# Taking the sorted experts of a mixture in the order narrow, wide, wide, narrow, wide, wide, narrow

## The chip, the cores and the metric

The kernel runs on one core of one Trainium2 chip. The metric is the device time of one execution in microseconds (us). Three runs of the kernel before gave 1553.4, 1556.64 and 1560.38 us; the median is 1556.64 us. The profiled execution took 1559.97 us, of which 1558.3 us lie between its first and its last instruction (the span).

## The reference

The program is a decoder trunk of two layers on 256 tokens of 1024 features, all in 32-bit floats. Each layer mixes the tokens (a gated convolution, a state-space model, two kinds of attention) and then mixes channels. The channel mixer of layer 0 is dense; the one of layer 1 sends each token to two of eight experts. Only that last part bears on the change:

```python
logits = (h @ router_w).astype(jnp.float32)
top_val, top_idx = lax.top_k(logits, 2)
top_w = jax.nn.softmax(top_val, axis=-1)
gate = jnp.sum(jax.nn.one_hot(top_idx, 8) * top_w[..., None], axis=-2)
for e in range(8):
    out = out + gate[..., e:e + 1] * swiglu(h, w_gate[e], w_up[e], w_down[e])
# swiglu(h, g, u, d) = (silu(h @ g) * (h @ u)) @ d, with 1024 -> 3584 -> 1024
```

The weights of one expert are 3 x 1024 x 3584 numbers of 4 bytes, which is exactly 42 MiB (44.04 MB); all eight are 336 MiB. Every expert's weights are read once, whatever the number of its tokens.

## The kernel before, in words

Layer 0 and the token mixing of layer 1 fill the first 630 us or so of the span; the change does not touch them. The mixture of experts is `moe`, and its main loop runs over eight places `e` (L1405).

**Sorting and sizes.** Place 0 is always expert 0. The other seven experts are sorted on the chip by the number of their tokens, fullest first (`sort`, L1325); `order["ids"]`, `order["sl"]` and `order["ge"]` hold their numbers, the places of their tokens and their gates in that order. Expert 0 and the first four of the sorted ones (`WIDE`) have room for 96 tokens, the last three for 64. A place with 96 is called wide here, and one with 64 narrow. Tokens beyond the room would go to a part behind the loop (`beyond`), which runs only where there are any.

**Gather.** `gather` (L1185) collects the tokens of one or more experts: a matrix of zeros and ones `So` is built by VectorE, and 32 matmuls (L1204) multiply it with the tokens (in a high and a low part), so that X holds the tokens' columns side by side. Expert 0 is gathered ahead of the loop, with 96 columns. Three joint gathers serve the rest: behind the third unit of place 0 (for two experts), of place 2 (for two) and of place 4 (for three).

**Units.** An expert's 3584 hidden features are worked in four units `u`: three of 1024 features and one of 512. `hidden` (L1243) takes eight steps `k` over the 1024 input features. In each step one load of 1 MiB (half a load in the last unit) is multiplied with X; TensorE's columns are used in four strips of 32 tokens, so a step has 12 matmuls on strips for a wide place (`ROUNDS[3]`) and 8 for a narrow one (`ROUNDS[2]`). A 32-bit matmul is two instructions in the trace, so 24 and 16 records. `finish` (L1387) is the second half of a unit: `turn` transposes the hidden features (L1275, and L1282 for wide), `down` (L1286) multiplies them with 14 loads of 1 MiB for each expert (L1306 for wide, L1299 for narrow), and behind the last unit `gated` and `scatter` add the result to the output `y` (L1215 to L1226). `finish` is a generator, and `step(k)` takes one piece of it behind each step of a later `hidden` (two pieces behind the last two steps). A place's units have 43 pieces in all and its steps take 40, so the pieces run late, by three more at each place; what is left at the end is run behind the last `hidden`.

**Loads.** `load` (L261) issues each MiB on SyncE's queue, in the order of the program, into a ring of twelve places: nine tiles `raw` and the tiles `yA`, `sp` and `mix`. A load waits until the last matmul on the place's old contents is done. Twelve loads are 12/42 of an expert.

**Banks.** PSUM has two banks `ps` and six banks `acc`. A wide place takes two `acc` banks for its output and three for a unit of `hidden`; a narrow one takes one and two. The compiler's scheduler assigns them as they come free.

Of the kernel before, what the change touches and what calls it, by code (L numbers as in the profile page):

```python
# [10 lines left out]
F32R = mybir.dt.float32r  # L11
# [6 lines left out]
T, D, E = 256, 1024, 8  # L18
KD = D // 128
NT = T // 128  # L20
WIDE = 4
PI = math.pi
MAGIC = 12582912.0
C1 = 6.28125
# [141 lines left out]
def trunk(ctx: ExitStack, tc: tile.TileContext, I, out):  # L166
    nc = tc.nc
# [7 lines left out]
    def nm(n):  # L175
        cnt[0] += 1
        return f"{n}_{cnt[0]}"

    def st(shape, tag, bufs=1, dt=F32):
        return sb.tile(shape, dt, tag=tag, bufs=bufs, name=nm(tag))  # L180

    def s2(shape, dt=F32):
        return st(shape, "s2", NS2, dt)

    def bank(tag="acc"):
        return ps.tile([128, 512], F32, tag=tag, bufs=NPS[tag], name=nm(tag))

    def ts(o, a, s1, s2=None, op0=OP.mult, op1=None, eng=None):
        if s2 is None:
            (eng or V).tensor_scalar(o, a, s1, None, op0=op0)  # L190
        else:
            (eng or V).tensor_scalar(o, a, s1, s2, op0=op0, op1=op1)

    def tt(o, a, b, op=OP.mult):
        return V.tensor_tensor(o, a, b, op=op)  # L195

    def stt(o, a, s, b, op0=OP.mult, op1=OP.add):
        return V.scalar_tensor_tensor(o, a, s, b, op0=op0, op1=op1)  # L198

    def act(o, a, f, **k):  # L200
        S.activation(o, a, f, **k)  # L201
# [4 lines left out]
    x = st([128, KD, T], "x")  # L206
# [10 lines left out]
    def C(n):  # L217
        o, w = CS[n]
        return cst[:, o:o + w]
# [20 lines left out]
    hpi = st([128, 1], "hpi")  # L240
    V.memset(hpi, PI / 2)

# [56 lines left out]
    def run(*gens):  # L299
        for g in gens:  # L300
            for _ in g:
                pass
# [98 lines left out]
    def reduce2pi(r, a, n):  # L401
        ts(n, a, 1.0 / (2 * PI), MAGIC, OP.mult, OP.add)
        ts(n, n, MAGIC, None, OP.subtract)
        stt(r, n, -C1, a)
        stt(r, n, -C2, r)
        ts(r, r, PI, -PI, OP.min, OP.max)

# [89 lines left out]
    def rstd(src_ss, n, width, scale):  # L497
        ms = st([128, n], "ms", 2)
        pn = src_ss.shape[0]
        m = ms[:pn, :width]  # L500
        ts(m, src_ss, scale, 1e-6, OP.mult, OP.add)
        G.tensor_tensor(m, m, mhalf[:pn, :width], op=OP.pow)
        return ms
# [47 lines left out]
    def norm(l, which, shift, scale, old=None, lo=0, hi=KD):  # L551
        gs = gain(l, which, scale, lo, hi)
        rB, ah, al = old or (scales()[0], st([128, KD, T], "ah", 1, F32R), st([128, KD, T], "al", 1, F32R))
        u = gained(gs, lo, hi)
        for k2 in range(lo // 2, hi // 2):
            tt(u[k2], u[k2], rB[:, None, :].to_broadcast([128, 2, T]))
            for kk in range(2):
                k = 2 * k2 + kk
                act(ah[:, k], u[k2][:, kk], AF.Identity, bias=shift[:, k:k + 1])
                last = stt(al[:, k], u[k2][:, kk], shift[:, k:k + 1], ah[:, k].bitcast(F32), OP.add, OP.subtract)  # L560
        return rB, ah, al, last.ins

    def hop(n, l):
        for _ in range(1 + PAUSE.get((n, l), 0)):
            yield
# [6 lines left out]
    def mixer(l, ah, al, extra=(), second=None, ahead=None):  # L572
# [48 lines left out]
        def s5():  # L621
# [11 lines left out]
            yield  # L633
            W = [bank(), bank()]
            for ri in range(2):
                for i in range(8):
                    PE.matmul(W[ri][:, i * 64:(i + 1) * 64], BT[:, ri, i], U[:, i], start=True, stop=True)
            yield from hop("s51", l)
            W = [w.rearrange("p (i j) -> p i j", i=8) for w in W]
            a0, a1, a2, a3 = (s2([128, 8, 64]) for _ in range(4))  # L640
            tt(a0, W[0], cT)
            tt(a1, W[1], sT)
            tt(a2, W[1], cT)
            tt(a3, W[0], sT)
# [122 lines left out]
        def rope_norm(dst, src, tabs, g, tmp):  # L767
# [4 lines left out]
            act(m1[:pn], src, AF.Square)  # L772
            V.tensor_reduce(ss[:pn, :n], m1[:pn], axis=AX.X, op=OP.add)
            r = rstd(ss[:pn, :n], 8, n, 1.0 / 64)
# [91 lines left out]
        def sparse():  # L866
# [15 lines left out]
            mx = st([128, NT, 4], "mx8")  # L882
            V.tensor_reduce(mx, sc, axis=AX.X, op=OP.max)
            tt(sc, sc, mx[:, :, :, None].to_broadcast(b4), OP.subtract)
            act(sc, sc, AF.Exp, scale=0.125)
            yield from hop("sparse1", l)
            tt(sc, sc, cm("cmpmul"))
            V.tensor_reduce(mx, sc, axis=AX.X, op=OP.add)
            ts(mx, mx, 1e-30, None, OP.max)
# [26 lines left out]
        def head(o, pov, pcT):  # L916
# [4 lines left out]
            for t in range(NT):  # L921
# [7 lines left out]
                m = st([128, 2], "m2", 4)  # L929
                V.tensor_reduce(m, sv, axis=AX.X, op=OP.max)  # L930
                ts(m, m, -0.125)
# [186 lines left out]
    def moe(l, shift, fill):  # L1118
# [29 lines left out]
        tt(g1, g1, g2, OP.add)  # L1148
        V.tensor_reduce(rk, g1, axis=AX.X, op=OP.add)
        sel = st([128, NT, E], "sel")  # L1150
        ts(sel, rk, 2.0, None, OP.is_lt)
        mx = st([128, NT], "mxr")
        V.tensor_reduce(mx, lg, axis=AX.X, op=OP.max)
        ge = st([128, NT, E], "ge")
# [10 lines left out]
        sl = st([128, NT, E], "sl")  # L1165
# [19 lines left out]
        def gather(jobs, So=None):  # L1185


            n = sum(c for _, c in jobs)
            if So is None:
                So = st([128, NT, 128], "cv", 2, F32R)  # L1190
            X = st([128, KD, 192], "xt", 2)
            at, got = 0, []
            for off, c in jobs:
                for t in range(NT):
                    ts(So[:, t, at:at + c], C("iota")[:, :c], off[:, t], None, OP.is_equal)
                got.append((X[:, :, at:at + c], So[:, :, at:at + c], c))
                at += c
            for k2 in range(KD // 2):
                p = bank("ps")
                for kk in range(2):  # L1200
                    c = slice((k2 * 2 + kk) * 128, (k2 * 2 + kk + 1) * 128)
                    for i, src in enumerate((ahi, alo)):
                        for t in range(NT):
                            PE.matmul(p[:, kk * n:(kk + 1) * n], src[:, t, c], So[:, t, :n],  # L1204
                                      start=(kk == 0 and i == 0 and t == 0), stop=(i == 1 and t == NT - 1),
                                      skip_group_check=True)
                act(X[:, k2 * 2:k2 * 2 + 2, :n], p[:, :2 * n].rearrange("p (a b) -> p a b", a=2), AF.Copy)
            return got
# [114 lines left out]
        order = {}  # L1323

        def sort():  # L1325
# [33 lines left out]
            V.memset(room[:, :1], 96.0)  # L1359
            ts(room[:, 1:], rank, float(WIDE), 32.0, OP.is_lt, OP.mult)  # L1360
            ts(room[:, 1:], room[:, 1:], 64.0, None, OP.add)
# [13 lines left out]
        def weights(e):  # L1375
            flat = lambda a: a.rearrange("o p a b -> (o p) a b")
            s = bass.ds(e, 1)
            return (lambda u, k: flat(wi[s, u, k]), lambda k2: flat(we[s, k2]),
                    lambda r: flat(wd.rearrange("(e r) p a b -> e r p a b", e=E)[s, r]))

        spare[:] = ["raw"] * RAW + ["yA", "sp", "mix"]
        got = {}
# [4 lines left out]
        def finish(W, u, h, acc, G, gate, So, c):  # L1387

            yield
            t = turn(*h, G)  # L1390
            yield
            yield from down(W, u, t, acc, G)
            if u == 3:
                ye = gated(acc, G)
                yield
                yield from scatter(gate, ye, So, c)
# [3 lines left out]
                if steps and next(steps[0], 0) == 0:  # L1400
                    steps.pop(0)

        places = [96] * (1 + WIDE) + [64] * (E - 1 - WIDE)
        groups = {0: (1, 2), 2: (3, 4), 4: (5, 6, 7)}
        for e in range(E):  # L1405
            X, So, c = got[e]
            G = c // 32
            gate = order["ge"][:, :, e - 1:e] if e else ge[:, :, :1]
            W = weights(0 if not e else nc.values_load(order["ids"][:1, e - 1:e], engines=[mybir.EngineType.SP],
                                                       min_val=1, max_val=E - 1))  # L1410
            acc = [bank() for _ in range(G - 1)]
            for u in range(4):
                h = hidden(W, u, X, G, step)
                steps.append(finish(W, u, h, acc, G, gate, So, c))
                if e == 0 and u == 0:
                    sort()
                if u == 2 and e in groups:
                    js = groups[e]
                    if not e:
                        chosen = st([128, len(groups), NT, 192], "x", 1, F32R)  # L1420
                    jobs = [(order["sl"][:, :, j - 1:j], places[j]) for j in js]
                    for j, o in zip(js, gather(jobs, chosen[:, e // 2])):
                        got[j] = o
        run(*steps)
        send()

# [115 lines left out]
    i = norm(0, "gmix", mod[0, 0], mod[0, 1], old, 0, 4)[3]  # L1542
# [68 lines left out]
```

## Time and profile before

| | |
|---|---|
| median of three runs | 1556.64 us |
| profiled execution | 1559.97 us |
| its span | 1558.3 us |
| TensorE busy (PE) | 1471.6 us, 94% of the span |
| DMA, share of 16 engines | 79.9% of the span |
| bytes read from HBM | 489.98 MB |

PE is TensorE's matmuls, PEld its weight loads, DVE VectorE, ACT ScalarE, SPq the queue of SyncE. The profile's page cuts the span into 40 equal slices of 39 us; the mixture's loop lies in the slices from the 17th on. The granted clock is given in tenths or as a share of 2.4 GHz. A group of matmuls is shown with the time from the start of its first to the end of its last; since matmuls are pipelined, the next group's start, and not this one's end, tells how long a group held the engine.

### The profile page before, as it was taken

What the parts mean: (1) busy time and instruction counts of PE and PEld (TensorE: products, weight loads), DVE (VectorE), ACT (ScalarE), POOL (GpSimd) and SP (SyncE); (2) the same over time, 40 slices, a digit from 0 to 9 for tenths busy, and PEclk for the clock granted to TensorE, in tenths of its full rate; (3) what the DMA queues carried; (4) which work ended last, traced back from release to release, by engine and by line L of the source; (5) the groups of instructions that cost most, each with busy time, mean ns of one, the idle gap of its engine ahead of it and who ended that gap; (6) DMA issues with size and microseconds to landing.
All of it is one profiled execution on the core that took longest, in us unless ns stands there. A gap on an engine that the chain in (4) does not pass through costs nothing.

```text
span 1558.3 us, 33641 instructions
## 1 busy us (share of the span) xinstructions
PE 1471.6 (94%) x14822; PEld 904.9 (58%) x14822; DVE 532.6 (34%) x1118; ACT 366.4 (24%) x636; POOL 38.5 (2%) x44
## 2 busy tenths in 40 slices
PE   6999989999999999899999999999999999787786
PEld 4888689999998987444534534544544543122121
DVE  7785568788557864210020020011001011010011
ACT  3437445444443563110000011010001000000010
POOL 1020000000000200000000000000000000000000
PEclk9999999999999999799999999999999999999999
DMA  9975534789654543499989999898998999999996
GB/s 384 380 307 196 197 118 183 271 295 333 236 180 183 232 163 108 166 374 396 349 338 398 382 381 352 335 413 335 385 393 344 354 420 420 421 420 421 420 421 253
DMA packets 69403, 493.30 MB, mean 317 GB/s; under 512 B 8320, under 2 KB 8320, under 8 KB 10240
## 3 DMA queue, kind: packets, MB, share of 16 engines
q1 hardware_dynamic: 69248, 491.06, 79.9%
q8 instruction: 118, 1.93, 0.5%
q14 instruction: 37, 0.30, 0.1%
HBM read 489.98 MB, written 1.05 MB: 315 GB/s over the span
## 4 chain that ended last, share of the span: by engine, by line
PE 76%; DMA 18%; DVE 4%; issue 1%; ACT 1%; POOL 0%; SPq 0%; DVEq 0%; ACTq 0%; POOLq 0%
PE acc L1256 25%; PE acc L1306 11%; DMA raw<-in_moe_w_in_dram 6%; PE ps L289 6%; PE ps L291 6%; PE ps L290 6%; DMA mix<-in_moe_w_down_dram 4%; DMA raw<-in_moe_w_down_dram 4%; PE acc L289 3%; PE acc L290 3%; PE acc L291 3%; DMA mix<-in_moe_w_in_dram 3%; DMA raw<-in_moe_w_end_dram 1%; PE ps L1204 1%; DVE s L195 1%
## 5 line engine op out<-in xcount | busy, mean ns | idle before, releaser
L1256 PE MATMUL acc<-raw,xt 128*32 128x512 f32 (+1 forms) x4008 | 432.7, 545 | 17.0 <-DMA raw<-in_moe_w_in_dram 15.8
L195 DVE TENSOR_TENSOR s<-acc,s 128x512 f32<-128x512 f32 (+6 forms) x91 | 53.7, 595 | 774.1 <-PE acc L1256 432.7
L1256 PEld LDWEIGHTS acc<-raw,xt 128*32 128x32 f32 x4008 | 135.6, 110 | 238.0 <-issue 162.1
L195 DVE TENSOR_TENSOR wl<-raw,wh 128x1024 fp32r<-128x1024 f32 x144 | 175.5, 1222 | 91.7 <-PE ps L291 52.4
L289 PE MATMUL ps<-ah,wh 128*128 128x256 f32 x672 | 193.8, 289 | 6.6 <-ACT ah L201 5.6
L290 PE MATMUL ps<-al,wh 128*128 128x256 f32 x672 | 191.9, 286 | 2.1 <-DVE al L198 2.1
L291 PE MATMUL ps<-ah,wl 128*128 128x256 f32 x672 | 192.2, 287 | 0.0
L201 ACT ACTIVATE wh<-raw 128x1024 fp32r<-128x1024 f32 x144 | 152.1, 1061 | 169.9 <-PE ps L290 101.8
L1306 PE MATMUL acc<-raw,s 128*32 128x256 f32 x2496 | 168.4, 379 | 0.0
L201 ACT ACTIVATE s<-acc 64x512 f32<-64x512 f32 (+5 forms) x93 | 47.4, 513 | 410.7 <-PE acc L1256 333.8
L289 PEld LDWEIGHTS ps<-ah,wh 128*128 128x128 f32 x672 | 129.7, 193 | 13.2 <-ACT ah L201 6.0
L1306 PEld LDWEIGHTS acc<-raw,s 128*32 128x32 f32 x2496 | 94.5, 110 | 69.2 <-issue 24.3
L290 PEld LDWEIGHTS ps<-al,wh 128*128 128x128 f32 x672 | 130.0, 194 | 2.7 <-DVE al L198 2.5
L291 PEld LDWEIGHTS ps<-ah,wl 128*128 128x128 f32 x672 | 129.9, 193 | 1.5 <-DVE s L198 0.8
L201 ACT ACTIVATE s<-ps 128x256 f32<-128x256 f32 (+3 forms) x95 | 42.4, 464 | 326.3 <-PE ps L1275 303.7
L1299 PE MATMUL acc<-raw,s 128*32 128x512 f32 x512 | 61.5, 598 | 15.2 <-DMA raw<-in_moe_w_down_dram 14.9
L289 PE MATMUL acc<-s,wh 128*128 128x256 f32 x224 | 63.2, 283 | 0.0
L290 PE MATMUL acc<-s,wh 128*128 128x256 f32 x224 | 63.1, 283 | 0.0
L291 PE MATMUL acc<-s,wl 128*128 128x256 f32 x224 | 62.7, 283 | 0.0
L201 ACT ACTIVATE s<-s 128x512 fp32r<-128x512 f32 (+6 forms) x50 | 28.5, 569 | 130.1 <-DVE s L195 124.4
L1256 PE MATMUL acc<-yA,xt 128*32 128x512 f32 (+1 forms) x488 | 55.2, 538 | 2.6 <-DMA yA<-in_moe_w_in_dram 2.6
L1256 PE MATMUL acc<-mix,xt 128*32 128x512 f32 (+1 forms) x464 | 52.7, 535 | 2.3 <-DMA mix<-in_moe_w_in_dram 1.7
(367 smaller groups left out, 1697.2 us busy)
## 6 DMA issues: line engine op xcount, KB each, us to landing
raw<-in_moe_w_in_dram SPq DMA_DIRECT2D x145, 1024.0 KB, 8.8
raw<-in_moe_w_down_dram SPq DMA_DIRECT2D x84, 1024.0 KB, 9.4
raw<-in_ada_w_dram SPq DMA_DIRECT2D x48, 1024.0 KB, 7.4
raw<-in_moe_w_end_dram SPq DMA_DIRECT2D x23, 1024.0 KB, 8.6
raw<-in_w_in_dram SPq DMA_DIRECT2D x18, 1024.0 KB, 7.8
yA<-in_moe_w_in_dram SPq DMA_DIRECT2D x17, 1024.0 KB, 9.2
mix<-in_moe_w_in_dram SPq DMA_DIRECT2D x16, 1024.0 KB, 8.9
raw<-in_ffn_w_gate_dram SPq DMA_DIRECT2D x14, 1024.0 KB, 4.8
```

Source lines behind the costliest of these rows:

```text
L195: return V.tensor_tensor(o, a, b, op=op)
L201: S.activation(o, a, f, **k)
L289: PE.matmul(o, lh, rh, start=start, stop=False, skip_group_check=True)
L290: PE.matmul(o, lh, rl, start=False, stop=False, skip_group_check=True)
L291: return PE.matmul(o, ll, rh, start=False, stop=stop, skip_group_check=True)
L1204: PE.matmul(p[:, kk * n:(kk + 1) * n], src[:, t, c], So[:, t, :n], start=(kk == 0 and i == 0 and t == 0), stop=(i == 1 and t == NT - 1), s ...
L1256: PE.matmul(bk[r][32 * j:32 * j + 32, :n], X[:, k, 32 * g:32 * g + 32], v[:, b_], start=(k == 0), stop=(k == KD - 1), skip_group_check=True)
L1299: PE.matmul(acc[0][32 * j:32 * j + 32], lhs[j % 2], v[:, c % 2, j // 2 * 512:j // 2 * 512 + 512], start=first, stop=last, skip_group_check ...
L1306: PE.matmul(o[32 * j:32 * j + 32], lhs[g], v[:, c % 2, q * 256:q * 256 + 256], start=first and r != 1, stop=last, skip_group_check=True)
```

## The change

The seven sorted experts are taken by the list `TURN`. The places' sizes, 96 first, are now wide, narrow, wide, wide, narrow, wide, wide, narrow; before they were five wide ones and then three narrow ones. The joint gathers take the experts of the next two, two and three places as before, but their columns are now 64 + 96 = 160, 96 + 64 = 160 and 96 + 96 + 64 = 256, where they were 192, 192 and 192. X and `So` have room for 256 columns in place of 192. Which expert has which room does not change, nor does the arithmetic of an expert.

```diff
+TURN = (4, 0, 1, 5, 2, 3, 6)
...
-            X = st([128, KD, 192], "xt", 2)
+            X = st([128, KD, T], "xt", 2)
...
-        places = [96] * (1 + WIDE) + [64] * (E - 1 - WIDE)
-        groups = {0: (1, 2), 2: (3, 4), 4: (5, 6, 7)}
+        groups = {0: (0, 1), 2: (2, 3), 4: (4, 5, 6)}
         for e in range(E):
             X, So, c = got[e]
             G = c // 32
-            gate = order["ge"][:, :, e - 1:e] if e else ge[:, :, :1]
-            W = weights(0 if not e else nc.values_load(order["ids"][:1, e - 1:e], engines=[mybir.EngineType.SP],
+            i = TURN[e - 1]
+            gate = order["ge"][:, :, i:i + 1] if e else ge[:, :, :1]
+            W = weights(0 if not e else nc.values_load(order["ids"][:1, i:i + 1], engines=[mybir.EngineType.SP],
                                                        min_val=1, max_val=E - 1))
...
-                        chosen = st([128, len(groups), NT, 192], "x", 1, F32R)
-                    jobs = [(order["sl"][:, :, j - 1:j], places[j]) for j in js]
+                        chosen = st([128, len(groups), NT, T], "x", 1, F32R)
+                    jobs = [(order["sl"][:, :, TURN[j]:TURN[j] + 1], 96 if TURN[j] < WIDE else 64) for j in js]
                     for j, o in zip(js, gather(jobs, chosen[:, e // 2])):
-                        got[j] = o
+                        got[j + 1] = o
```

## Rows read from the trace of the kernel before

**Rows 1.** The page, 40 slices of the span: granted TensorE clock in tenths, DMA rate.
```profile
PEclk9999999999999999799999999999999999999999
...
GB/s 384 380 307 196 197 118 183 271 295 333 236 180 183 232 163 108 166 374 396 349 338 398 382 381 352 335 413 335 385 393 344 354 420 420 421 420 421 420 421 253
```

**Rows 2.** Busy time in stretches of 20 us: early and late in the loop.
```profile
core 0: us, PE busy (x) PEld busy (x) DVE busy (x) ACT busy (x) POOL busy (x), PEclk, DMA share, GB/s
...
700.00:720.00 20.00, 20.00 (x228) 7.53 (x220) 1.39 (x2) 2.06 (x4) 0.00 (x0) 1.00 1.01 422
...
1440.00:1460.00 20.00, 15.84 (x138) 3.48 (x130) 0.69 (x1) 1.47 (x3) 0.00 (x0) 1.00 1.01 421
```

**Rows 3.** The same columns, the loop's wide and narrow stretches.
```profile
648.00:1266.00 618.00, 617.47 (x7586) 287.19 (x7578) 58.88 (x123) 54.64 (x111) 0.00 (x0) 1.00 0.94 372
1266.00:1546.50 280.50, 234.12 (x2192) 68.50 (x2182) 24.43 (x39) 17.33 (x35) 0.00 (x0) 1.00 0.99 411
```

**Rows 4.** The chain that ended last: shares; pieces by start and length (us).
```profile
PE 76%; DMA 18%; DVE 4%; issue 1%; ACT 1%; POOL 0%; SPq 0%; DVEq 0%; ACTq 0%; POOLq 0%
...
735.53 1.96 PE ps L1204 x16
...
1463.56 20.22 DMA mix<-in_moe_w_in_dram
...
1544.49 1.97 PE acc L1299 x16
```

**Rows 5.** Timeline of TensorE, a wide place: start us, us, engine, line, operation.
```profile
686.50 2.76 PE L1256 MATMUL acc<-raw,xt 128*32 128x512 f32 x24
689.08 1.48 PE L1306 MATMUL acc<-raw,s 128*32 128x256 f32 x24
690.37 2.76 PE L1256 MATMUL acc<-raw,xt 128*32 128x512 f32 x24
...
712.41 0.66 PE L1275 MATMUL ps<-cst,s 128*128 128x128 f32 x4
...
713.39 2.78 PE L1256 MATMUL acc<-mix,xt 128*32 128x512 f32 x24
```

**Rows 6.** The same view: one of a scatter's four pairs of matmuls, and its follower.
```profile
801.29 0.50 PE L1225 MATMUL ps<-s,k 96*128 96x512 f32 x1
...
801.96 1.06 PE L1256 MATMUL acc<-raw,xt 128*32 128x512 f32 x6
```

**Rows 7.** The same view: the last unit of a wide place, then a narrow one.
```profile
1225.96 1.50 PE L1256 MATMUL acc<-raw,xt 128*32 128x256 f32 x24
1227.25 1.50 PE L1306 MATMUL acc<-yA,s 128*32 128x256 f32 x24
...
1229.84 1.92 PE L1256 MATMUL acc<-mix,xt 128*32 128x512 f32 x16
1231.56 1.50 PE L1306 MATMUL acc<-sp,s 128*32 128x256 f32 x24
```

**Rows 8.** The same view, late in the narrow stretch; idle time before in brackets.
```profile
1451.06 1.92 PE L1256 MATMUL acc<-sp,xt 128*32 128x512 f32 x16 [0.56 <-DMA sp<-in_moe_w_in_dram]
1453.55 1.92 PE L1299 MATMUL acc<-mix,s 128*32 128x512 f32 x16 [0.57 <-DMA mix<-in_moe_w_down_dram]
```

**Rows 9.** DMA: issues between 700 and 1260 us; the rate between 1300 and 1540.
```profile
raw<-in_moe_w_in_dram SPq DMA_DIRECT2D x87, 1024.0 KB, 8.1
...
DMA packets 13794, 100.57 MB, mean 419 GB/s; under 512 B 1532, under 2 KB 1532, under 8 KB 1532
```

**Rows 10.** What SyncE's queue waited for, 640 to 1560: total us, times, longest.
```profile
SPq L264 <- PE acc L1256: 325.2, 137, 7.9
...
SPq L264 <- DMA raw<-in_moe_w_in_dram: 73.5, 38, 2.4
```

**Rows 11.** Timeline of TensorE: expert 0's gather of 96 columns, and its follower.
```profile
643.36 0.42 PE L1204 MATMUL ps<-cv,ah 128*128 128x96 f32 x2
...
644.38 3.66 PE L358 MATMUL ps<-raw,cond 128*32 128x256 f32 x64
```

## The prediction

> **What bounds the kernel now.** I read the page's slices first, then the busy times of stretches, the chain, the timeline of TensorE at single steps, the DMA view and the waits of SyncE's queue. In the slices [rows 1] the loop falls in two: from the 18th to the 32nd slice the DMA moves 335 to 413 GB/s, and from the 33rd to the last but one 420 or 421. The stretches say why. From 648 to 1266 us, the five wide places and the start of the first narrow one, TensorE is busy for 617.47 of 618 us while the DMA moves 372 GB/s; from 1266 to the last matmul of `down` TensorE is busy for 234.12 of 280.5 us while the DMA is full [rows 3]. The chain ends accordingly in DMA pieces of some 20 us, and the DMA has 18% of it [rows 4]. So wide places are bound by TensorE and narrow ones by the DMA, and each limit lies idle where the other holds. The granted clock is 1.00 in the first stretch and 0.99 in the second [rows 3]: the clock is at its upper level of 2.4 GHz throughout, and the narrow stretch's short waits do not lower it.
>
> **What one place costs.** For TensorE I take start to start. A wide step of `hidden` with 512 columns takes 689.08 - 686.50 = 2.58 us, and the piece of `down` behind it 690.37 - 689.08 = 1.29 [rows 5]; a wide step with 256 columns takes 1227.25 - 1225.96 = 1.29, a narrow step with 512 takes 1231.56 - 1229.84 = 1.72 [rows 7]. A narrow step of 256 is half of that, 0.86, as it is for wide ones, and so is a narrow piece of `down`, which has 8 records of 512 columns where the step has 16. A wide turn takes 713.39 - 712.41 = 0.98 [rows 5], a narrow one without the second set of transposes some 0.6, and a scatter four times 801.96 - 801.29 = 0.67 [rows 6].
> Wide: 24 x 2.58 + 8 x 1.29 + 28 x 1.29 + 4 x 0.98 + 4 x 0.67 = 61.9 + 10.3 + 36.1 + 3.9 + 2.7 = 115 us. Narrow: 24 x 1.72 + 8 x 0.86 + 28 x 0.86 + 4 x 0.6 + 2.7 = 41.3 + 6.9 + 24.1 + 2.4 + 2.7 = 77 us.
> For the DMA a place costs 42 loads whatever its width: 1.0486 MB at 419 GB/s [rows 9] is 2.50 us a load, 105 us a place. A wide place is 10 us longer on TensorE than on the DMA, a narrow one 28 us shorter.
>
> **The change part by part.**
> *The order.* It removes no work: 336 loads, five wide and three narrow places, the same steps. What it can save is TensorE's idle time of the narrow stretch. That is 280.5 - 234.1 = 46 us by busy time [rows 3]. But a group of 16 records shows as 1.92 us busy and holds the engine for 1.72: in the narrow stretch loads come 1453.55 - 1451.06 = 2.49 us apart with 0.57 us shown idle, where 2.49 - 1.72 = 0.77 is free [rows 8]. Scaled by 0.77/0.57 the idle time is 62 us. The groups that do not wait need no such correction, so I take the middle, 55 us, with 46 and 62 as bounds.
> The Trainium skill, "Trainium Kernel Development and Optimization", section Performance Expectations, says that matmul busy time is a bad measure because matmuls are pipelined. The pair 1.92 and 1.72 agrees. By that rule alone the 62 would stand and the time would come out 7 us lower than below; by busy time alone 9 us higher.
> The DMA's unused time in the wide stretch is 618 x (1 - 372/419) = 69 us, which is more, so TensorE's idle time limits the gain.
> *What idle time stays.* A narrow place can use TensorE fully only with loads landed ahead. In the wide stretch a load is issued when the place of the twelfth load before it comes free: SyncE's queue waits there for L1256, 325.2 us in all [rows 10]. It lands 8.1 us later [rows 9]. Twelve loads last TensorE 12 x 115/42 = 33 us, so a load has landed some 25 us early, which is 9 loads. In a narrow place TensorE uses a load every 77/42 = 1.84 us and one lands every 2.50: nine loads are used up after 9 / (1/1.84 - 1/2.50) = 63 us, 34 loads, and the remaining 8 cost 0.66 each, 5 us. Two wide places behind it win 2 x 10 = 20 us back, 8 loads; the next narrow place then waits for 12 x 0.66 = 8 us, and the last one too. That makes 21 us. Against it stands that `finish` runs late: a narrow place first executes the last unit's pieces of the wide one before it, and three more per place, so some 3, 7 and 11 us of wide work move into places 1, 4 and 7, against waits of 5, 8 and 8. That leaves 3 us. Between 3 and 21 I take 8, nearer to the lower one because the late pieces stand in the code.
> *The gathers.* Three joint gathers of 32 matmuls stay, with 160, 160 and 256 columns for three times 192. At 192 columns 16 take 1.96 us [rows 4], 0.122 each, at 96 eight take 1.02, 0.128 each [rows 11]: flat over that range, so I take nothing. If they went with the columns, the two small ones would save 32 x 0.02 = 0.65 us each and the large one would cost 32 x 0.041 = 1.3. The copies of X out of PSUM are on ScalarE, busy for 54.64 of 618 us [rows 3]; 2 x 256 floats fill a `ps` bank and need no second one. VectorE builds the same number of matrices with the same widths. Where that cover is gone, TensorE stands before the next place for one copy, under 1 us.
> *Queues and banks.* SyncE's queue issues the same loads with the same number of reads of an expert's number; nothing waits that did not wait. For `acc` banks, a wide place behind a wide one asks for 2 + 3 + 2 = 7 of six until the older output is scattered. That occurs four times before and TensorE does not stand there [rows 3]; it occurs twice now. Narrow then wide asks for 1 + 3 + 2 = 6.
> *The end.* The last place is narrow in both. The last load lands, then 1.97 us of matmuls follow [rows 4], and the 15.5 us from 1544.49 to 1559.97 stay.
> **Sum:** 55 - 8 = 47 us. 1559.97 - 47 = 1513 for the profiled execution, which is 3.3 us above the median of the runs shown; on the median 1510 us. With the bounds: 46 - 21 = 25 gives 1532, 62 - 3 = 59 gives 1498.
>
> **The rivals.**
> *A short lead, 1544 us.* In the narrow stretch the queue waits for the landing eight loads back: a DMA piece of the chain takes 20.22 us, eight loads of 2.50 [rows 4], and 73.5 us of waits name a load [rows 10]. If eight were the depth everywhere, the lead would be 8 x 2.74 - 8.1 = 14 us, 5.5 loads, used up after 21; the other 21 cost 14 us in each narrow place, 42 in all, and the gain is 13. Against it: where TensorE is the limit, the queue waits for TensorE's release and not for a landing.
> *No change, 1557 us.* The DMA cannot run full beside a full TensorE, so no lead is won in wide places and every narrow place takes 105 us as before. Against it: between 700 and 720 us the DMA moves 422 GB/s while TensorE is busy for 20.00 of 20 us, as much as the 421 beside a waiting one [rows 2]. The lower mean of the wide stretch then comes from the ring.
> The Trainium skill, "DMA: Bandwidth & Descriptors", section Where 436 GB/s comes from, states that the HBM side, some 358 GB/s for a core, binds a load. As an estimate from that page a load would take 2.93 us and a place 123, more than a wide place's matmuls; every place would wait for the DMA in any order and this rival would hold. The 422 and 419 GB/s here disagree, and the measurement decides.
> *Slower, from banks at narrow then wide.* Places 1 to 2 and 4 to 5 need six of six banks. If the scheduler gave a bank to the new place's output before the old one is scattered, the first unit's third bank would be missing, and TensorE, which takes its queue in order, would stand up to a wide unit, 8 x 2.58 + 8 x 1.29 = 31 us. Two such stops are 62 against 47 gained: 1572 us. It decides from 24 us per stop. Against it: four places with a demand of seven pass without idle time [rows 3].
> That the order is not taken (all counts beyond their room, so that the part behind the loop runs) is excluded by the chain, which ends in the loop, and by rooms that go with the rank as before.
>
> **How the numbers follow.** The forecast holds with 0.86, the short lead with 0.08, no change with 0.03, slower with 0.03. 0.5% is 8 us, about what a measurement of this kernel tells from no change. Forecast and short lead are faster by more than that: 0.94. The range 1498 to 1530 takes in nearly all of the forecast's own bounds and leaves the rivals out.
>
> **What would show it.** In the changed profile: the rate is even over the loop, some 405 to 420 GB/s in nearly all slices, with no block of 420 at the end; TensorE's idle time between 648 us and the last `down` is under 20 us, in the last third of place 1 and near the ends of the other narrow ones, put down to DMA; the DMA's share of the chain falls from 18% to under 8%; matmuls of L1204 have forms of 160 and 256 columns at 0.12 us each; the loop ends about 47 us earlier, the granted clock stays at 1.00, and the tail is 15 us. Wrong would be: idle time of TensorE at the first unit of places 2 and 5 put down to banks (ACT or DVE on `acc`), waits in every narrow place of 14 us or more (short lead), or a load period over 2.6 us while TensorE is full.

## The result, and the profile after

The changed kernel took 1507.94 us in the median of 4 runs (1505.81 to 1510.18), against 1556.11 for the kernel before beside it (4 runs): a ratio of 0.9688, 95% interval 0.9661 to 0.9715. Forecast were 1510 us within 1498 to 1530. The profiled execution took 1506.84 us, where 1513 had been forecast for it.

The page of the changed kernel, its slices now 37.6 us long (lines as in rows 1) and the chain's shares (as in rows 4):

```profile
PEclk9999999999999999799999999999999999999998
...
GB/s 382 406 309 202 175 144 183 267 264 320 287 179 223 224 166 59 113 348 395 344 407 421 421 419 420 419 420 357 401 420 421 420 421 419 420 420 396 420 420 259
...
PE 84%; DMA 9%; DVE 4%; issue 1%; ACT 1%; POOL 0%; SPq 0%; DVEq 0%; ACTq 0%; POOLq 0%
```

The block of 420 GB/s no longer begins at the 33rd slice [rows 1] but at the 22nd, with two dips: the 28th and 29th slices and the 37th. Place 0 is still below it (344 to 395). The DMA's share of the chain has fallen from 18% [rows 4] to 9%.

For the loop by itself I measure from 10 us after the first matmul of `hidden` to the landing of the last load. First the changed kernel, then the kernel before; the columns are those of rows 2: length, TensorE busy and so on, clock, DMA share, GB/s.

```profile
646.00:1491.10 845.10, 833.84 (x9748) 361.01 (x9740) 82.91 (x161) 71.86 (x145) 0.00 (x0) 1.00 1.00 408
```

```profile
649.00:1544.40 895.40, 848.66 (x9744) 355.00 (x9736) 83.29 (x161) 71.59 (x145) 0.00 (x0) 1.00 0.96 385
```

895.4 - 845.1 = 50.3 us of the 53.1 between the two executions. The other 2.8 lie ahead of the loop: its first matmul starts at 636.05 us instead of 638.85. The code there is the same, and this start lies between 633 and 642 us in the profiles below; so loops are compared by their own length.

The same columns for four stretches of the changed loop that hold all but 0.5 us of its idle time: the end of place 1, the end of place 4, the wide places 5 and 6, and the last narrow place.

```profile
820.00:880.00 60.00, 55.92 (x564) 18.04 (x560) 6.32 (x10) 4.67 (x9) 0.00 (x0) 1.00 1.01 420
...
1100.00:1160.00 60.00, 58.01 (x618) 24.20 (x611) 8.21 (x14) 8.01 (x16) 0.00 (x0) 1.00 1.01 420
1160.00:1420.00 260.00, 260.00 (x3106) 113.62 (x3102) 22.95 (x36) 18.20 (x37) 0.00 (x0) 1.00 1.01 417
1420.00:1491.10 71.10, 66.45 (x743) 24.80 (x734) 8.29 (x14) 6.00 (x13) 0.00 (x0) 1.00 0.97 401
```

TensorE stands idle for 4.1, 2.0, 0 and 4.6 us, around the ends of the three narrow places. In the third row both limits are met at once: TensorE busy for 260 of 260 us and the DMA at 417 GB/s.

Not all of this is loads. Two pieces of the timeline at the end of place 4 (start, length, idle time before and what ended it), and two around the end of place 1:

```profile
1145.43 0.66 PE L1276 MATMUL ps<-cst,s 128*128 128x128 f32 x4 [0.89 <-DVE s L196]
...
1158.89 0.44 PE L1276 MATMUL ps<-cst,s 128*128 128x128 f32 x2 [0.62 <-DVE s L196]
```

```profile
872.70 1.93 PE L1300 MATMUL acc<-raw,s 128*32 128x512 f32 x16 [0.72 <-DMA raw<-in_moe_w_down_dram]
875.20 2.78 PE L1257 MATMUL acc<-yA,xt 128*32 128x512 f32 x24 [0.57 <-DMA yA<-in_moe_w_in_dram]
```

In place 4 the idle time is that of a narrow place's `turn`, which waits for VectorE's product of the hidden features. Over the whole loop loads end 6.9 us of the idle time (1.8, 0.6 and 0.4 on L1257 by the tile loaded, 2.4, 0.6, 0.6 and 0.5 on L1300) and VectorE 4.3 (3.3 on L1276, 1.0 on L1227). In the kernel before it was 42.7 us for loads, in 72 waits against 13 now, and 3.4 for VectorE.

The lead itself, how long before its use a load has landed, can be read on `yA`, which takes every twelfth load. Two of its loads in the changed kernel, one of place 3 and one around the end of place 1 (first and last start of the matmuls that read it, time of issue, time to landing):

```profile
L1257 PE MATMUL acc<-yA,xt x7: 592/592/592, 1046.4 to 1047.3; 128*32 128x512 f32 x7
L265 SPq DMA_DIRECT2D yA<-in_moe_w_in_dram x1: 333/333/333, 1014.6 to 1014.6; - x1
...
DMA to landing us min/median/max: 11.6/11.6/11.6
```

```profile
L1257 PE MATMUL acc<-yA,xt x12: 592/592/617, 875.2 to 876.1; 128*32 128x512 f32 x12
...
L265 SPq DMA_DIRECT2D yA<-in_moe_w_in_dram x1: 332/332/332, 854.3 to 854.3; - x1
...
DMA to landing us min/median/max: 20.9/20.9/20.9
```

The first has landed 1046.4 - 1014.6 - 11.6 = 20.2 us ahead of its use, the second not at all. Read in this way, the lead falls to nothing around the end of place 1, is back at 20 us in place 3, falls to 1.2 us at 1214, where late pieces of place 4 still run, is back at 16 us at 1381, and is gone at 1486. In the kernel before it is 10.6 to 28.0 us over the wide places (21.6 in the median of 17 loads used between 707 and 1251 us), and at most 1.0 us from 1328 on.

The chain's end, as in rows 4 (start, length):

```profile
1471.35 19.71 DMA mix<-in_moe_w_down_dram
...
1491.11 1.97 PE acc L1300 x16
```

The last load lands, 1.97 us of matmuls follow, and 15.7 us are left to the execution's end, as forecast.

### The profile page after: what moved, and what is told of

Its sections match the earlier page's. It is cut to its first block, busy times and chain, and to the rows that moved or that the text cites. A ratio compares the mean times of both kernels' runs of the same rounds, so it can differ in the third digit from the quotient of the medians.

```text
span 1505.0 us, 33629 instructions
## 1 busy us (share of the span) xinstructions
PE 1454.5 (97%) x14822; PEld 910.2 (60%) x14822; DVE 532.1 (35%) x1118; ACT 366.8 (24%) x636; POOL 38.5 (3%) x44
## 4 chain that ended last, share of the span: by engine, by line
PE 84%; DMA 9%; DVE 4%; issue 1%; ACT 1%; POOL 0%; SPq 0%; DVEq 0%; ACTq 0%; POOLq 0%
PE acc L1257 30%; PE acc L1307 12%; PE ps L290 6%; PE ps L292 6%; PE ps L291 6%; PE acc L290 3%; PE acc L291 3%; PE acc L292 3%; DMA raw<-in_moe_w_down_dram 3%; DMA raw<-in_moe_w_end_dram 3%; PE acc L1300 2%; DMA yA<-in_moe_w_in_dram 1%; DMA mix<-in_moe_w_down_dram 1%; PE ps L1205 1%; DVE s L196 1%
## 5 line engine op out<-in xcount | busy, mean ns | idle before, releaser
L1257 PE MATMUL acc<-raw,xt 128*32 128x512 f32 (+1 forms) x3992 | 425.0, 545 | 1.8 <-DMA raw<-in_moe_w_in_dram 1.2
L1257 PEld LDWEIGHTS acc<-raw,xt 128*32 128x32 f32 x3992 | 138.9, 110 | 207.8 <-issue 168.6
L1307 PE MATMUL acc<-raw,s 128*32 128x256 f32 x2688 | 173.9, 379 | 0.0
L1307 PEld LDWEIGHTS acc<-raw,s 128*32 128x32 f32 x2688 | 98.5, 110 | 76.4 <-issue 30.4
L1300 PE MATMUL acc<-raw,s 128*32 128x512 f32 x448 | 57.2, 595 | 2.4 <-DMA raw<-in_moe_w_down_dram 2.4
L1257 PE MATMUL acc<-yA,xt 128*32 128x512 f32 (+1 forms) x480 | 53.5, 537 | 0.6 <-DMA yA<-in_moe_w_in_dram 0.6
L1257 PE MATMUL acc<-mix,xt 128*32 128x512 f32 (+1 forms) x464 | 51.5, 535 | 0.4 <-DMA mix<-in_moe_w_in_dram 0.4
## 6 DMA issues: line engine op xcount, KB each, us to landing
raw<-in_moe_w_in_dram SPq DMA_DIRECT2D x145, 1024.0 KB, 14.7
```

The source lines that it names most:

```text
L1257: PE.matmul(bk[r][32 * j:32 * j + 32, :n], X[:, k, 32 * g:32 * g + 32], v[:, b_], start=(k == 0), stop=(k == KD - 1), skip_group_check=True)
L1300: PE.matmul(acc[0][32 * j:32 * j + 32], lhs[j % 2], v[:, c % 2, j // 2 * 512:j // 2 * 512 + 512], start=first, stop=last, skip_group_check ...
L1307: PE.matmul(o[32 * j:32 * j + 32], lhs[g], v[:, c % 2, q * 256:q * 256 + 256], start=first and r != 1, stop=last, skip_group_check=True)
```

## The experiments

The theory: a wide place leaves the DMA time to run ahead, a narrow one uses that lead up, and the ring's places limit it; so the order decides. The rivals: tiles and gathers; banks, or wide places directly behind wide ones; a loop at the DMA's floor. Each ratio is against the kernel before, run beside it (median 1553.8 to 1555.9 us).

**1. The old order in the changed kernel.**

```diff
-TURN = (4, 0, 1, 5, 2, 3, 6)
+TURN = (0, 1, 2, 3, 4, 5, 6)
```

> The changed kernel with the sorted experts taken in the old order, wide ones first; X and So keep room for 256 columns and the joint gathers have 192 columns again. Theory (the order alone decides, through loads landed ahead in the ring): the old time, 1556 us, within 5. Rival (the smaller first gathers or the wider tiles carry the gain): 1508 us, the changed kernel's time, or something between.

Measured: 1554.01 us, ratio 0.9990 (0.9972 to 1.0007). Tiles for 256 places and the indexing by `TURN` cost nothing that shows; the order carries the gain.

**2 and 3. Nine places in the ring, in the changed kernel and in the one before.**

```diff
-        spare[:] = ["raw"] * RAW + ["yA", "sp", "mix"]
+        spare[:] = ["raw"] * RAW
```

> The changed kernel with nine places in the ring of loads in place of twelve (yA, sp and mix are not used for expert weights). Theory (narrow places live on the lead that the ring holds): nine places hold 9 x 2.74 - 8.1 = 17 us of lead, 6.6 loads, used up after 46 us; stepping the 42 loads of each place through the prices of the prediction gives 20 us more than with twelve, 1528 us (1520 to 1534). Rival (alternation as such, by fewer wide places behind wide ones and their banks): the ring hardly matters, 1508 to 1516 us.

> The kernel before with nine places in the ring in place of twelve. Theory: the lead is used only once, at the step from wide to narrow, and for loads ahead of the loop, so three places fewer cost three loads of 2.5 us, 7.5 us: 1564 us (1560 to 1567), a third of what they cost the changed kernel. Rival (a short ring slows every wide place too, since loads come late): the same 20 us as in the changed kernel, 1576 us.

Measured: 1524.73 us, ratio 0.9813 (0.9774 to 0.9852), for the changed order; 1563.16 us, ratio 1.0045 (1.0027 to 1.0062), for the old one. Three places are worth 17 us to the changed order and 7 to the old one; by the loops' own lengths it is 863.1 - 845.1 = 18.0 and 900.1 - 895.4 = 4.7. The loop with nine places, changed order and then old order:

```profile
643.00:1506.10 863.10, 837.91 (x9728) 357.87 (x9720) 82.92 (x161) 71.87 (x145) 0.00 (x0) 1.00 0.99 402
```

```profile
646.00:1546.10 900.10, 848.99 (x9736) 353.75 (x9727) 83.28 (x161) 71.60 (x145) 0.00 (x0) 1.00 0.97 386
```

TensorE's idle time grows from 11.3 to 25.2 us in the changed order, and from 46.7 to 51.1 in the old. In the old order the wide places are full with nine as well, so a late load does not slow them:

```profile
700.00:1200.00 500.00, 500.00 (x6127) 231.54 (x6122) 48.01 (x78) 41.63 (x86) 0.00 (x0) 1.00 0.95 370
```

**4 to 6. Fifteen places.** The tiles `wh` and `wl` of the dense part become pairs of 1 MiB, which can join the ring in the loop. Run 5 leaves out the last line below, and run 6 has the old `TURN` of run 1 besides.

```diff
-RAW, WH, WL, NS2 = 9, 4, 3, 11
+RAW, WH, NS2 = 9, 3, 11
...
-        hi = st([128, 1024], "wh", WH, F32R)
-        lo = st([128, 1024], "wl", WL, F32R)
+        hl = st([128, 2048], "wh", WH, F32R)
+        hi, lo = hl[:, :1024], hl[:, 1024:]
...
-        spare[:] = ["raw"] * RAW + ["yA", "sp", "mix"]
+        spare[:] = ["raw"] * RAW + ["yA", "sp", "mix"] + ["wh"] * WH
```

> The changed kernel; the dense part's tiles wh (four) and wl (three) become three pairs of one 1 MiB tile each, and in the loop these three are added to the ring, which has 15 places. Theory (lead decides): no narrow place waits and three more loads come in ahead of the loop; stepping gives 6 to 12 us less, 1496 to 1502 us, if three wh tiles in place of four cost the dense part nothing. Rival (the loop is already bound by the DMA's rate alone): 1506 to 1510 us, or more where the dense part gets slower.

> The changed kernel with the dense part's tiles wh and wl as three pairs, and the ring still of twelve places. It tells what the pairs by themselves cost or give. If the ring's three more places made the gain of the run with fifteen: 1508 us or a little above. If the pairs change the dense part: another time, and the ring's share is the difference to 1498 us.

> The kernel of the run with fifteen places in the ring, with the old order of the places, wide ones first. Theory: three more places give three loads of 2.5 us once, as three fewer cost it: 7 to 8 us under the old order with twelve, 1546 to 1549 us. Rival (a deep ring makes the order matter less, and narrow places in a row live on it): 1530 us or less.

Measured: 1498.15 us, ratio 0.9623 (0.9586 to 0.9660), with fifteen places; 1508.45 us, ratio 0.9700 (0.9667 to 0.9734), with the pairs and twelve. The pairs cost nothing that shows (the loop takes 845.1 us, as in the changed kernel), and three more places give 10 us. This version beats both kernels. Its loop, and the end of place 1 where the changed kernel waited for 4.1 us:

```profile
650.00:1484.50 834.50, 830.65 (x9740) 362.30 (x9732) 82.93 (x161) 71.87 (x145) 0.00 (x0) 1.00 1.00 409
```

```profile
820.00:880.00 60.00, 60.00 (x603) 20.75 (x602) 6.64 (x10) 5.27 (x10) 0.00 (x0) 1.00 1.01 420
```

Idle time is down to 3.9 us, 3.7 of it put down to VectorE and none to a load, and none is left in place 1. In the old order fifteen places gave 1551.83 us, ratio 0.9983 (0.9965 to 1.0001), 3 us above what was expected. Its loop is shorter than in run 1 by 894.1 - 888.1 = 6.0 us, near the 7.5 expected, but starts at 638.80 us instead of 633.42. Old order in run 1, then with fifteen places:

```profile
643.00:1537.10 894.10, 847.51 (x9732) 354.58 (x9724) 83.30 (x161) 71.56 (x145) 0.00 (x0) 1.00 0.96 385
```

```profile
649.00:1537.10 888.10, 847.99 (x9744) 356.04 (x9736) 83.38 (x161) 71.71 (x145) 0.00 (x0) 1.00 0.96 384
```

**7 and 8. Two other orders.**

```diff
-TURN = (4, 0, 1, 5, 2, 3, 6)
+TURN = (4, 0, 5, 1, 6, 2, 3)   # run 7: wide, narrow, wide, narrow, wide, narrow, wide, wide
+TURN = (0, 1, 2, 4, 5, 3, 6)   # run 8: wide x 4, narrow, narrow, wide, narrow
```

> The changed kernel with the places wide, narrow, wide, narrow, wide, narrow, wide, wide; joint gathers of 160, 160 and 256 columns. Theory: narrow places are fed as before, so the last load lands 3 to 5 us earlier than in the changed kernel, but the last two wide places leave TensorE behind the loads, and late pieces of a wide place follow the last step; stepping gives 19 us more than the changed kernel, 1527 us (1518 to 1532). Rival (each wide place directly behind a wide one costs, some 24 us each by the four before and the two now): only one such pair is left, 1484 us.

> The changed kernel with the places wide, wide, wide, wide, narrow, narrow, wide, narrow. Theory: the lead is capped by the ring, so three of the four first wide places win nothing beyond it, and the second narrow place in a row has no lead left and takes the DMA's 105 us; stepping gives 34 us more than the changed kernel, 1542 us (1534 to 1548). Rival (24 us for each wide place directly behind a wide one): three such pairs, 1532 us.

Measured: 1518.86 us, ratio 0.9775 (0.9739 to 0.9811), and 1538.62 us, ratio 0.9891 (0.9855 to 0.9927). Both lie in the theory's ranges, 8 and 3 us under its values, and against the rival by 35 and 7 us. Run 8 alone does not exclude the rival, since its interval, 1531 to 1542 us, still takes in the rival's 1532; run 7 does: it has only one wide place behind a wide one and is slower than the changed kernel with two. In run 7 the last load lands early, at 1481.5 us, and TensorE's end is what is left over (the stretch before that landing, and the one behind it):

```profile
1460.00:1481.50 21.50, 21.20 (x381) 13.50 (x382) 0.85 (x2) 2.01 (x5) 0.00 (x0) 1.00 0.77 312
1481.50:1516.90 35.40, 25.92 (x394) 14.65 (x386) 6.67 (x11) 3.00 (x7) 0.00 (x0) 0.87 0.10 34
```

35.4 us instead of 14 follow the last landing. In run 8 the two narrow places in a row give the picture of the old order's end, 13.9 of 80 us idle:

```profile
1220.00:1300.00 80.00, 66.13 (x616) 19.46 (x616) 7.37 (x11) 4.79 (x9) 0.00 (x0) 1.00 1.01 421
```

**9 and 10. All narrow and all wide**, each limit by itself.

```diff
-                    jobs = [(order["sl"][:, :, TURN[j]:TURN[j] + 1], 96 if TURN[j] < WIDE else 64) for j in js]
+                    jobs = [(order["sl"][:, :, TURN[j]:TURN[j] + 1], 64) for j in js]   # all narrow; place 0 too
+                    jobs = [(order["sl"][:, :, TURN[j]:TURN[j] + 1], 96) for j in js]   # all wide
```

> Leaves work out: every expert has room for 64 tokens, so tokens beyond that in the fuller experts are dropped. It prices the DMA alone: 42 loads of 2.5 us at each of eight places with TensorE waiting. Theory: the DMA never waits, the last load lands some 19 us earlier than in the changed kernel, 1489 us (1483 to 1495). That is the floor of any order with twelve places. Rival (the changed kernel is already at the DMA's floor): 1505 to 1510 us.

> Every expert has room for 96 tokens (more work than needed, with four joint gathers of 192, 192, 192 and 96 columns). It prices TensorE alone: a wide place by itself. Theory: no place waits for loads, and each of the three places that were narrow costs some 38 us more of TensorE than in the changed kernel, less the idle time that was left: 1617 us (1608 to 1626). Rival (wide places cost the DMA's 105 us or so when the DMA can run ahead): below 1580 us.

Measured: 1481.35 us, ratio 0.9535 (0.9487 to 0.9582), 2 us below the range expected, and 1620.58 us, ratio 1.0419 (1.0383 to 1.0456). The loop of the one, and 800 us of the other:

```profile
648.00:1466.30 818.30, 676.97 (x6134) 198.61 (x6127) 64.89 (x126) 53.72 (x105) 0.00 (x0) 1.00 1.01 418
```

```profile
700.00:1500.00 800.00, 800.00 (x9892) 374.09 (x9888) 74.31 (x121) 67.34 (x141) 0.00 (x0) 1.00 0.94 369
```

With TensorE unloaded the DMA keeps 418 GB/s over the loop and needs 818.3 us; the changed kernel's 845.1 is 27 above that floor. Three places made wide cost 1620.58 - 1507.94 = 113 us. That is less than their matmuls take, because the changed kernel's 11 us of idle time went with it. TensorE from the loop's first matmul to the last one, here and in run 4:

```profile
638.40:1612.90 974.50, 970.36 (x12053) 452.25 (x12052) 99.24 (x189) 85.50 (x178) 0.00 (x0) 1.00 0.90 355
```

```profile
639.60:1492.40 852.80, 846.54 (x9867) 368.90 (x9866) 87.86 (x169) 74.17 (x150) 0.00 (x0) 1.00 0.98 402
```

The busy times differ by 124 us; without the fourth gather's 4 us that is 40 for each place, where the prediction's prices of 115 and 77 us differ by 38. And 970.36 us less four gathers is some 119 us for a wide place, where it had 115.

**11. Late pieces on time.**

```diff
-            for _ in range(1 + (k > 5)):
+            for _ in range(1 + (k > 4)):
```

> The changed kernel with two pieces of finish behind the last three steps of a unit, where it had two behind the last two, so that a place's steps take 44 pieces where its units have 43, and pieces are at most a unit late. It tests the step of the prediction by which late wide pieces shorten the waits of narrow places from 21 to 3 us. By that step places 4 and 7 lose most of their 7 and 11 us of wide work and the waits come back: 1513 to 1520 us. Rival (the waits are short anyway, since the two wide places in between refill the ring; stepping every load through the prices gives 1 us more): 1506 to 1511 us.

Measured: 1507.59 us, ratio 0.9702 (0.9677 to 0.9728): the changed kernel's time. The same stretches as above, ends of the places 1, 4 and 7:

```profile
820.00:880.00 60.00, 56.43 (x560) 18.73 (x556) 8.06 (x12) 5.27 (x10) 0.00 (x0) 1.00 1.01 420
1100.00:1160.00 60.00, 58.23 (x550) 21.69 (x546) 8.66 (x14) 7.51 (x13) 0.00 (x0) 1.00 1.02 421
...
1420.00:1491.90 71.90, 66.72 (x646) 21.90 (x638) 8.14 (x14) 5.88 (x12) 0.00 (x0) 1.00 0.99 410
```

3.6, 1.8 and 5.2 us idle, against 4.1, 2.0 and 4.6. Over the whole loop loads end 4.5 us of it (6.9 before) and VectorE 6.8 (4.3): pieces more than a unit late do not shorten the waits for loads.

## Why the prediction was right, step by step

**The bound** held: TensorE in wide places, the DMA in narrow ones. So did the load of 2.50 us. **The prices** of a place on TensorE were low: some 119 us for a wide place and 40 less for a narrow one (run 10 beside run 4), where the sum had 115 and 77, and the 4 us of a joint gather, in places 0, 2 and 4, stood in no place's price.

**The idle time to be won was put too low.** I took 55 us, the middle between 46 by busy time and 62 by start to start [rows 3, 8]. The loop got 50.3 us shorter while its idle time by busy time fell only from 46.7 to 11.3, by 35.4. The other 14.9 us are busy time that vanished, 848.66 to 833.84, with the same 14822 matmuls in the execution. Most of it is the 0.2 us by which a group that waits shows longer than it holds the engine: TensorE's waits in the loop fell from 79 to 20, and 59 x 0.2 = 12 us. The remaining 3 were not traced. What was won and what stayed make 50.3 + 11.3 = 61.6 us at the least, where I had taken 55. The rule of the Trainium skill ("Trainium Kernel Development and Optimization", Performance Expectations) that matmul busy time is a bad metric was right against my middle value; the upper bound of 62 agrees.

**The idle time that stayed** was put at 8 us, between 3 and 21, all of it for loads. Loads take 6.9, as forecast around the ends of places 1 and 7, and none in place 4; the other 4.3 are waits for VectorE, in `turn` above all, which the prediction had not set apart from the idle time to be won. The reason I gave for going near the lower end fell: by run 11 the late pieces do not shorten the waits for loads. What does was not isolated. The prices point to it: two wide places of 119 us win 2 x 14 = 28 us back, not 20, and with a gather of 4 us each in places 2 and 4, place 4 comes out without a wait, as measured. No run takes these terms away. Besides, a place's last unit of `finish` runs in the next place in both kernels, which moves some wide work into each narrow place. The two errors, 7 us of idle time too few and 3 left too few, partly cancel, which is luck: 47 was forecast, 50.3 came.

**The lead** as a ring of twelve, less a load's way, was the step on which everything hung, and runs 2 to 6 bear it out: nine places lose 17 us and fifteen win 10 in the new order, where the old order changes by 7 and 4. The nine places part the orders best; by the loops alone fifteen win 10.6 and 6.0 us. The lead read on `yA` is 21.6 us where 25 was forecast. The time and the effect of the depth settle the rival with a depth of eight, which gave 1544. (That rival took its 14 us as 5.5 loads, at 2.50 us each, where the forecast took its 25 as 9, at 2.74. By 2.74 it is 5 loads and some 1547 us, no nearer to the result.)

**The gathers at nothing.** TensorE's timeline of the large joint gather: start, length as before.

```profile
1128.88 0.39 PE L1205 MATMUL ps<-x,al 128*128 128x256 f32 x2
1129.12 0.40 PE L1205 MATMUL ps<-x,ah 128*128 128x256 f32 x2
```

Two matmuls of 256 columns hold the engine for 0.24 us, 0.12 each, as at 192 columns [rows 4]. All 32 take 4.2 us where they took 3.9, so the wider gather costs 0.3 us and not the 1.3 by columns.

**No change, and slower by banks.** Beside a full TensorE the DMA moves 417 GB/s for 260 us, so a core alone is not held to the 358 GB/s of "DMA: Bandwidth & Descriptors", section Where 436 GB/s comes from, in the Trainium skill. For banks, the stretches at the two steps from narrow to wide show 4.1 and 2.0 us idle in all, none behind the second (1160 to 1420 us), not 24 and more for each, put down to loads and to VectorE's product, not to a bank.

**The signs.** Of what was to show it, TensorE's idle time under 20 us, the clock at 1.00, 0.12 us for a gather's matmul and the tail came. Two did not. The rate is not even: it is 344 to 395 GB/s in place 0 and mostly 420 from place 1 to the end. And the DMA's share of the chain is 9%, not under 8%. The even rate did not follow from the forecast's own argument: in place 0 the ring is full, as in the wide places before, and once place 1 draws on the lead, the DMA runs at its full rate until the lead is back, around the dips of the 28th and 29th slices and of the 37th.

## What to carry to other kernels

Where stages of a loop have different limits, and each limit lies idle in the other's stages, put the stages in turn so that what one leaves over is stored as landed loads for the other: the store is the ring's depth, and the lead it holds (places times the compute time of a load, less a load's way) should cover what one short stage uses up. Price a waiting TensorE by start to start of its groups, not by busy time, in which 15 of the 50 us won here did not show as idle. End with a stage that leaves little compute behind its last load: the order with wide places last (run 7), counted from the first matmul of its loop, had its last load 6.8 us earlier and ended 14.7 us later.

## What the runs showed that was not expected

The start of the loop moved between 633 and 642 us over profiles of kernels whose code ahead of it is the same or nearly so; a few us of difference between two medians have to be read from the loop.
